# Merging the halves of 32x32 inverses: two (chunk, head) units in one 64x64 product, of which the diagonal blocks are kept

## The chip, the core and the metric

The kernel runs on one core of one Trainium2 chip. The core has a matrix engine (TensorE, "PE" in the profile, with its weight loads listed apart as "PEld"), a vector engine (VectorE, "DVE"), a scalar engine (ScalarE, "ACT"), a general engine (GpSimd, "POOL") and an engine that issues transfers (SyncE, "SP"). Each works through its own queue of instructions, and an instruction waits on semaphores for the results it needs. Matrix products are written to PSUM, here eight banks of 512 float32 columns by 128 partitions; ACT and DVE copy them out to SBUF.

The metric is the time of one execution on the device in microseconds, the median over the runs.

## The reference, cut to what matters

One layer of a hybrid decoder on 256 tokens of width 2048: a pooling mixer and an RWKV-7 time mixing side by side, an output projection, a squared-ReLU MLP and a gated embedding. The change lies in the time mixing, whose core is this recurrence over tokens, for 16 heads of size 64:

```python
def step(S, inp):
    r_t, w_t, k_t, v_t, a_t, b_t = inp
    sa = jnp.einsum('bhij,bhj->bhi', S, a_t)
    S = S * w_t[:, :, None, :] + sa[..., None] * b_t[:, :, None, :] + v_t[..., None] * k_t[:, :, None, :]
    y = jnp.einsum('bhij,bhj->bhi', S, r_t)
    return S, y
```

## The kernel before, in words

**Chunks instead of tokens.** The recurrence is computed in chunks of 64 tokens. Within a chunk, the products of all tokens with each other (the scores, tile SC) form a triangular 64x64 system per chunk and head, and its inverse is needed. The 16 heads are split into two groups, `gi` 0 and 1, of 8 heads; with 4 chunks each group has 32 (chunk, head) units.

**The inverse.** `inverse` works on a group at once. The 64x64 triangle of a unit is cut into two 32x32 diagonal blocks and one 32x32 block beside them. Both diagonal blocks lie on partitions 0 to 31 and 32 to 63: ACT copies them into `tmp` (L612), DVE transposes them into `AT` (L616), 31 steps of two DVE instructions build the inverses in `X` (L621, L625), and DVE transposes the results into `T1G` (L630, first block) and back into `tmp` (L634), from where ACT puts them into SC (L638). It is a generator: `pace` runs a step of it each time that TensorE's covering work has advanced by a given estimate.

**The merge.** `rwkv_merge` makes the block beside the diagonal. The first products, PSUM tile `gm`, multiply the score block SC[0:32, unit, 32:64] with the first inverse T1G[0:32, unit]; ACT copies the result to T1G[32:64] (L650). The second products, `qm`, multiply that with the second inverse, and ACT copies the result into SC (L657). Each is 32 products of 32x32 on 32 rows, one per unit, in two banks of 16.

**Order.** TensorE's instructions stay in the order in which the program is written (`manual_schedule` for PE alone). The other engines' queues are ordered by a scheduler from the dependencies and priorities. Between the dependent steps of the time mixing `fill(us)` puts products of the large projections, estimated in microseconds, as cover: `fill(1.5)` stands between gm and qm, and comes out as nine products of 128x512. Around the merge the program runs, for group 0: values of group 0, fill, scores of group 1 (`rwkv_scores`, L572, masked out of the banks by DVE at L579), merge of group 0, start of group 1's inverse, fill, core of group 0. For group 1: the pooling mix (`pool_mix`, L870 on ACT and L871 on DVE), merge, values, fill, core.

**Buffers.** The tiles of the time mixing come from a pool with one buffer per tag, so a tile waits until the last reader of the one before it in its tag is done. In group 0, `AT` and then `T1G` have the tag q0, `X` has q1, `tmp` q2; the values' tiles UV (written by ACT at L670 from the banks `vt`) use q0 and q1 after them. The small PSUM tiles (`rw_bank`: values, scores, gm, qm, core) share four banks. The large projections have four others. Weights are loaded by SP in tiles `raw`, split by ACT (L151, two halves) and DVE (L152, the difference) into `wh` and `wl`, three buffers each.

Of the kernel before, what the change touches and what calls it, by code (L numbers as in the profile page):

```python
# [9 lines left out]
F32 = mybir.dt.float32  # L10
F32R = mybir.dt.float32r
AF = mybir.ActivationFunctionType
# [28 lines left out]
def trunk(  # L41
# [19 lines left out]
    nc = tc.nc  # L61
# [11 lines left out]
    def rw_bank(name):  # L73
        return psr.tile([128, 512], F32, tag="rw", name=name)
# [159 lines left out]
    def fill(us):  # L234

        while us > 0 and queue:
            us -= advance()
# [42 lines left out]
    rp = rctx.enter_context(tc.tile_pool(name="rp", bufs=1))  # L280
# [58 lines left out]
    for kg, (tg, n) in enumerate((("tE", 1), ("tF", 2), ("zk", 3), ("zr", 3), ("zv", 3), ("BK", 2), ("BKt", 2))):  # L339
# [13 lines left out]
        if kg == 4:  # L353
            for tt in range(2):
                for i, q in enumerate((2, 3)):
                    nc.tensor.matmul(
                        sbank[:, tt : tt + 1], sums[q][:, 0, tt * 128 : (tt + 1) * 128], ones[:, 0:1],
                        start=i == 0 and tt == 0, stop=i == 1, skip_group_check=True,
# [242 lines left out]
    def inverse(gi, st):  # L601


        SC = st["SC"]
        SCu = SC[:, 0].rearrange("s c h t -> s (c h) t")
        tags = ("tB", "tD", "tE") if gi else ("q0", "q1", "q2")
        AT, X, tmp = (
            rp.tile([64, 32, 32], F32, tag=tg, name=f"{nm}{gi}") for nm, tg in zip(("AT", "X", "tmp"), tags)
        )
        for q in range(2):  # L610
            r = slice(q * 32, q * 32 + 32)
            nc.scalar.activation(tmp[r], SCu[r, :, q * 32 : q * 32 + 32], AF.Copy)  # L612
        nc.gpsimd.memset(X, 0.0)
        nc.gpsimd.memset(X.rearrange("u j t -> u (j t)")[:, ::33], 1.0)
        yield
        nc.vector.transpose(AT.rearrange("u s t -> u t s"), tmp.rearrange("s u t -> s t u"))  # L616
        yield
        for k in range(31):
            n, m = k + 1, 31 - k
            t_ = tmp.rearrange("u j t -> u (j t)")[:, 0 : n * m].rearrange("u (j t) -> u j t", t=m)  # L620
            nc.vector.tensor_tensor(  # L621
                t_, X[:, 0:n, k : k + 1].to_broadcast([64, n, m]),
                AT[:, k, n:32].unsqueeze(1).to_broadcast([64, n, m]), op=ALU.mult,
            )
            nc.vector.tensor_tensor(X[:, 0:n, n:32], X[:, 0:n, n:32], t_, op=ALU.add)  # L625
            yield
        T1G = rp.tile([64, 32, 32], F32, tag=tags[0], name=f"T1G{gi}")
        for hf in range(2):
            h = slice(hf * 16, hf * 16 + 16)
            nc.vector.transpose(T1G[0:32].rearrange("t u j -> t j u")[:, h], X[0:32][:, h])  # L630
            yield
        for hf in range(2):
            h = slice(hf * 16, hf * 16 + 16)
            nc.vector.transpose(tmp.rearrange("j u t -> j t u")[:, h], X.rearrange("u j t -> u t j")[:, h])  # L634
            yield
        for q in range(2):
            r = slice(q * 32, q * 32 + 32)
            nc.scalar.activation(SCu[r, :, q * 32 : q * 32 + 32], tmp[r], AF.Copy)  # L638
        st["T1G"] = T1G
        yield  # L640

    def rwkv_merge(gi, st):
        SC, T1G = st["SC"], st["T1G"]
        SCu = SC[:, 0].rearrange("s c h t -> s (c h) t")
        for hf in range(2):
            b = rw_bank("gm")
            for u in range(16):
                uu = hf * 16 + u
                nc.tensor.matmul(b[32:64, u * 32 : u * 32 + 32], SCu[0:32, uu, 32:64], T1G[0:32, uu, :], start=True, stop=True)
            nc.scalar.activation(T1G[32:64, hf * 16 : hf * 16 + 16].rearrange("t u j -> t (u j)"), b[32:64, :], AF.Copy)  # L650
        fill(1.5)
        for hf in range(2):
            b = rw_bank("qm")
            for u in range(16):
                uu = hf * 16 + u
                nc.tensor.matmul(b[0:32, u * 32 : u * 32 + 32], T1G[32:64, uu, :], SCu[32:64, uu, 32:64], start=True, stop=True)
            nc.scalar.activation(  # L657
                SCu[0:32, hf * 16 : hf * 16 + 16, 32:64], b[0:32, :].rearrange("j (u t) -> j u t", t=32), AF.Copy
            )

    def rwkv_values(gi, st, zv):

# [236 lines left out]
    fill(7.0)  # L899
    rwkv_scores(0, st0)  # L900
    beside += [inverse(0, st0), 1.65, 0.0]
    rwkv_sources(0, st0)
    finish(p_zv0)
# [8 lines left out]
    fill(7.0)  # L912
    rwkv_scores(1, st1)
    rwkv_merge(0, st0)
    beside += [inverse(1, st1), 0.95, 0.0]
    fill(1.5)
    core0 = rwkv_core(0, st0)
# [9 lines left out]
    run(beside.pop(0) if beside else ())  # L927
    beside.clear()
    rwkv_merge(1, st1)
    rwkv_values(1, st1, zv1[0])  # L930

# [423 lines left out]
```

## Time and profile before

| | |
|---|---|
| Median of 3 runs | 1205.03 us (1204.11 to 1207.36) |
| The profiled execution: span from its first to its last instruction | 1198.9 us; its own device time isn't listed, and the runs lie 5.2 to 8.5 us above this span |
| PE busy | 1179.6 us, 98% |
| PE weight loads busy | 1013.6 us, 85% |
| DVE, ACT, POOL busy | 72%, 57%, 1% |
| gm and qm products (L649, L656) | 128 records each, 191 ns each, overlapping |
| ACT copies of gm and qm (L650, L657) | 4 each, 0.59 us each |
| Scalar copy of a 32x1024 block (L612) | 1.06 us |

In the profile's timelines a row gives the start, the duration, the engine, the line, the operation, and the tile written and the tiles read; "x64" means that many records in a row, whose duration is then that of the whole stretch. In the rows by stretch, the busy time and the count of records of PE, PEld, DVE, ACT and POOL stand in that order, then the granted TensorE clock as a share of full speed, the share of the transfer engines and the GB/s.

### The profile page before, as it was taken

To read this page: it belongs to the slowest core of one execution; us is meant where nothing else is said; L and a number is where in the kernel's file an instruction comes from. 1 tells how busy PE (TensorE), PEld (TensorE's weight loads), DVE (VectorE), ACT (ScalarE), POOL (GpSimd) and SP (SyncE) were. 2 spreads that over 40 slices of the span, in tenths; PEclk is the share of its full clock that TensorE was granted. 3 is DMA by queue.
4 is the path that set the end of the run, shared out by engine and by line. 5 is a ranking of instruction groups with operands and counts; after the bars stand their busy time and mean duration, and the time that the engine had idled before them with its cause. 6 is when DMAs were issued, how large, how long until landed. Compare 5 with 4: busy or idle time off the path is not lost.

```text
span 1198.9 us, 18442 instructions
## 1 busy us (share of the span) xinstructions
PE 1179.6 (98%) x7076; PEld 1013.6 (85%) x7076; DVE 868.1 (72%) x1150; ACT 687.7 (57%) x1260; POOL 15.4 (1%) x65
## 2 busy tenths in 40 slices
PE   8999999999999999999999999999999999999996
PEld 6999988988888888888888788888888888778886
DVE  8687987854556667666888878666667888887552
ACT  6857565665545556555555555555555655668544
POOL 4000000000000000000000000000000000000000
PEclk9999999999999999999999999999999999999999
DMA  7463542354355565666665666665565655776631
GB/s 250 151 202 110 173 155 95 121 186 142 116 177 169 185 185 191 192 193 189 194 203 197 197 197 203 195 187 189 192 193 178 211 198 191 290 234 219 194 121 71
DMA packets 60328, 216.88 MB, mean 181 GB/s; under 512 B 6736, under 2 KB 7120, under 8 KB 59856
## 3 DMA queue, kind: packets, MB, share of 16 engines
q1 hardware_dynamic: 59952, 215.19, 55.1%
q8 instruction: 55, 0.90, 0.3%
q10 hardware_dynamic: 288, 0.52, 0.1%
q14 instruction: 33, 0.27, 0.1%
HBM read 213.59 MB, written 2.10 MB: 180 GB/s over the span
## 4 chain that ended last, share of the span: by engine, by line
PE 81%; DMA 6%; DVE 6%; ACT 4%; issue 2%; SPq 0%; ACTq 0%; DVEq 0%
PE u_w L986 20%; PE u_w L990 10%; DMA raw_d<-in_w_ffn_down_dram 5%; PE d_b L1101 4%; PE d_b L1100 4%; PE d_b L1102 4%; PE gt_b L173 2%; PE gt_b L175 2%; PE gt_b L174 2%; PE zv_b L164 1%; PE zp_b L173 1%; PE wag_b L333 1%; PE zv_b L165 1%; PE zv_b L166 1%; PE zp_b L175 1%
## 5 line engine op out<-in xcount | busy, mean ns | idle before, releaser
L986 PE MATMUL u_w<-h,wh_u 128*128 128x512 f32 x1024 | 355.4, 393 | 0.0
L990 PE MATMUL u_w<-h,wl_u 128*128 128x256 f32 x1024 | 285.5, 279 | 0.0
L151 ACT ACTIVATE wh_u<-raw_u 128x512 fp32r<-128x512 f32 x256 | 147.6, 624 | 162.9 <-PE u_w L986 82.0
L152 DVE TENSOR_TENSOR wl_u<-raw_u,wh_u 128x1024 fp32r<-128x1024 f32 x128 | 156.6, 1224 | 112.1 <-ACT wh_u L151 112.1
L986 PEld LDWEIGHTS u_w<-h,wh_u 128*128 128x128 f32 x1024 | 191.8, 187 | 43.2
L990 PEld LDWEIGHTS u_w<-h,wl_u 128*128 128x128 f32 x1024 | 193.1, 189 | 0.1
L152 DVE TENSOR_TENSOR wl_gt<-raw_gt,wh_gt 128x1024 fp32r<-128x1024 f32 x24 | 29.4, 1225 | 23.9 <-ACT wh_gt L151 23.9
L151 ACT ACTIVATE wh_gt<-raw_gt 128x512 fp32r<-128x512 f32 x48 | 27.8, 631 | 23.0 <-PE gt_b L175 20.4
L1140 DVE TENSOR_TENSOR td<-raw_d 128x512 f32<-128x512 f32 x22 | 15.2, 692 | 33.9 <-DMA raw_d<-in_w_ffn_down_dram 33.9
L164 PE MATMUL zv_b<-hTh,wh_zv 128*128 128x256 f32 x128 | 37.7, 294 | 0.0
L173 PE MATMUL gt_b<-wh_gt,h 128*128 128x512 f32 x96 | 37.5, 390 | 0.0
L164 PE MATMUL zr_b<-hTh,wh_zr 128*128 128x256 f32 x128 | 37.5, 293 | 0.0
L175 PE MATMUL gt_b<-wh_gt,h 128*128 128x512 f32 x96 | 37.4, 389 | 0.0
L174 PE MATMUL gt_b<-wl_gt,h 128*128 128x512 f32 x96 | 37.4, 389 | 0.0
L166 PE MATMUL zr_b<-hTh,wl_zr 128*128 128x256 f32 x128 | 37.2, 290 | 0.1
L164 PE MATMUL zk_b<-hTh,wh_zk 128*128 128x256 f32 x128 | 37.0, 289 | 0.0
L165 PE MATMUL zr_b<-hTl,wh_zr 128*128 128x256 f32 x128 | 36.9, 288 | 0.0
L165 PE MATMUL zk_b<-hTl,wh_zk 128*128 128x256 f32 x128 | 36.3, 284 | 0.5 <-DVE hTl L157 0.5
L166 PE MATMUL zk_b<-hTh,wl_zk 128*128 128x256 f32 x128 | 36.3, 284 | 0.2 <-DVE wl_zk L152 0.2
L166 PE MATMUL zv_b<-hTh,wl_zv 128*128 128x256 f32 x128 | 36.2, 283 | 0.0
L165 PE MATMUL zv_b<-hTl,wh_zv 128*128 128x256 f32 x128 | 36.2, 283 | 0.0
L156 ACT ACTIVATE wad<-raw_d 128x512 fp32r<-128x512 f32 x22 | 13.9, 632 | 36.6 <-DMA raw_d<-in_w_ffn_down_dram 34.5
(804 smaller groups left out, 3081.4 us busy)
## 6 DMA issues: line engine op xcount, KB each, us to landing
raw_u<-in_w_ffn_up_dram SPq DMA_DIRECT2D x128, 512.0 KB, 3.5
raw_d<-in_w_ffn_down_dram SPq DMA_DIRECT2D x128, 512.0 KB, 4.2
raw_gt<-in_w_ple_gate_dram SPq DMA_DIRECT2D x24, 512.0 KB, 3.5
raw_zk<-in_w_in_dram SPq DMA_DIRECT2D x16, 512.0 KB, 3.3
raw_zr<-in_w_in_dram SPq DMA_DIRECT2D x16, 512.0 KB, 3.3
raw_zv<-in_w_in_dram SPq DMA_DIRECT2D x16, 512.0 KB, 3.3
raw_zp<-in_w_in_dram SPq DMA_DIRECT2D x16, 512.0 KB, 3.2
raw_o<-in_w_out_dram SPq DMA_DIRECT2D x16, 512.0 KB, 3.5
```

Of the source, the lines that this page charges most:

```text
L151: nc.scalar.activation(wh[:, a * 512 : (a + 1) * 512], raw[:, a * 512 : (a + 1) * 512], AF.Copy)
L152: nc.vector.tensor_tensor(wl, raw, wh.bitcast(F32), op=ALU.subtract)
L164: nc.tensor.matmul(o, w_h, ah, start=first and ct % 2 == 0, stop=False, skip_group_check=True)
L165: nc.tensor.matmul(o, w_h, al, start=False, stop=False, skip_group_check=True)
L166: nc.tensor.matmul(o, w_l, ah, start=False, stop=last, skip_group_check=True)
L173: nc.tensor.matmul(o, a_h, wh[:, 0:n], start=first, stop=False)
L174: nc.tensor.matmul(o, a_h, wl[:, 0:n], start=False, stop=False)
L175: nc.tensor.matmul(o, a_l, wh[:, 0:n], start=False, stop=last)
L986: nc.tensor.matmul(bank[:, ct, :].rearrange("p (s t) -> p s t", s=2), wh[:, c], hl, start=k == 0, stop=False, skip_group_check=True,)
L990: nc.tensor.matmul(bank[:, ct, 0:T], wl[:, c], hl[:, 0, :], start=False, stop=k == 15, skip_group_check=True)
L1100: nc.tensor.matmul(banks[n], ah, wh, start=first, stop=False)
L1101: nc.tensor.matmul(banks[n], ah, wl, start=False, stop=False)
```

## The change

The merge takes two units per product. The left operand holds two 32x32 blocks side by side (64 columns), the right operand too, so the 64x64 result holds the two wanted products on its diagonal and two unwanted ones beside it. 16 products cover the 32 units, in one bank: even ones on partitions 0 to 63, odd ones on 64 to 127, eight column ranges of 64 each. Four copies then take the diagonal blocks out: block row r goes to every fourth unit from r on; r 0 and 2 are copied by ACT, 1 and 3 by DVE, 32 partitions by 8x32 elements each.

So that two neighbouring units lie side by side, the score block is first copied by ACT to a place of its own, `A12`, on partitions 64 to 95 of X's buffer (tiles of 96 partitions instead of 64); the first inverse's transposition goes to T1G[64:96] beside it.

```diff
@@ -605,8 +605,11 @@
         SCu = SC[:, 0].rearrange("s c h t -> s (c h) t")
         tags = ("tB", "tD", "tE") if gi else ("q0", "q1", "q2")
         AT, X, tmp = (
-            rp.tile([64, 32, 32], F32, tag=tg, name=f"{nm}{gi}") for nm, tg in zip(("AT", "X", "tmp"), tags)
+            rp.tile([96, 32, 32], F32, tag=tg, name=f"{nm}{gi}") for nm, tg in zip(("AT", "X", "tmp"), tags)
         )
+        A12, AT, X, tmp = X[64:96], AT[0:64], X[0:64], tmp[0:64]
+        nc.scalar.activation(A12, SCu[0:32, :, 32:64], AF.Copy)
+        st["A12"] = A12
         for q in range(2):
             r = slice(q * 32, q * 32 + 32)
             nc.scalar.activation(tmp[r], SCu[r, :, q * 32 : q * 32 + 32], AF.Copy)
@@ -624,10 +627,10 @@
             )
             nc.vector.tensor_tensor(X[:, 0:n, n:32], X[:, 0:n, n:32], t_, op=ALU.add)
             yield
-        T1G = rp.tile([64, 32, 32], F32, tag=tags[0], name=f"T1G{gi}")
+        T1G = rp.tile([96, 32, 32], F32, tag=tags[0], name=f"T1G{gi}")
         for hf in range(2):
             h = slice(hf * 16, hf * 16 + 16)
-            nc.vector.transpose(T1G[0:32].rearrange("t u j -> t j u")[:, h], X[0:32][:, h])
+            nc.vector.transpose(T1G[64:96].rearrange("t u j -> t j u")[:, h], X[0:32][:, h])
             yield
         for hf in range(2):
             h = slice(hf * 16, hf * 16 + 16)
@@ -642,21 +645,30 @@
     def rwkv_merge(gi, st):
         SC, T1G = st["SC"], st["T1G"]
         SCu = SC[:, 0].rearrange("s c h t -> s (c h) t")
-        for hf in range(2):
-            b = rw_bank("gm")
-            for u in range(16):
-                uu = hf * 16 + u
-                nc.tensor.matmul(b[32:64, u * 32 : u * 32 + 32], SCu[0:32, uu, 32:64], T1G[0:32, uu, :], start=True, stop=True)
-            nc.scalar.activation(T1G[32:64, hf * 16 : hf * 16 + 16].rearrange("t u j -> t (u j)"), b[32:64, :], AF.Copy)
+        A12 = st["A12"]
+
+        def block_products(name, left, right, place):
+
+            b = rw_bank(name)
+            for q in range(16):
+                u = slice(2 * q, 2 * q + 2)
+                nc.tensor.matmul(
+                    b[q % 2 * 64 : q % 2 * 64 + 64, q // 2 * 64 : q // 2 * 64 + 64], left(u), right(u),
+                    start=q < 2, stop=True, skip_group_check=True,
+                )
+            for r in range(4):
+                src = b[r * 32 : r * 32 + 32].rearrange("t (m j) -> t m j", j=64)[:, :, r % 2 * 32 : r % 2 * 32 + 32]
+                if r % 2:
+                    nc.vector.tensor_copy(place[:, r::4], src)
+                else:
+                    nc.scalar.activation(place[:, r::4], src, AF.Copy)
+
+        def two(t_):
+            return t_.rearrange("u b j -> u (b j)")
+
+        block_products("gm", lambda u: two(A12[:, u]), lambda u: two(T1G[64:96, u]), T1G[32:64])
         fill(1.5)
-        for hf in range(2):
-            b = rw_bank("qm")
-            for u in range(16):
-                uu = hf * 16 + u
-                nc.tensor.matmul(b[0:32, u * 32 : u * 32 + 32], T1G[32:64, uu, :], SCu[32:64, uu, 32:64], start=True, stop=True)
-            nc.scalar.activation(
-                SCu[0:32, hf * 16 : hf * 16 + 16, 32:64], b[0:32, :].rearrange("j (u t) -> j u t", t=32), AF.Copy
-            )
+        block_products("qm", lambda u: two(T1G[32:64, u]), lambda u: SCu[32:64, u, 32:64], SCu[0:32, :, 32:64])
 
     def rwkv_values(gi, st, zv):
 
```

## The prediction

> **What bounds the kernel now.** First the page: the busy times and the chain that ended last.
>
> ```profile
> PE 1179.6 (98%) x7076; PEld 1013.6 (85%) x7076; DVE 868.1 (72%) x1150; ACT 687.7 (57%) x1260; POOL 15.4 (1%) x65
> ...
> PE 81%; DMA 6%; DVE 6%; ACT 4%; issue 2%; SPq 0%; ACTq 0%; DVEq 0%
> ```
>
> TensorE has work almost all the time and carries four fifths of the chain. Second, the view of waits, for PE alone, longest first:
>
> ```profile
> PE wag_b L333 <- ACT tA_t L314: 5.0, 1, 5.0
> PE h3t L1007 <- DVE x L1120: 1.3, 1, 1.3
> ```
>
> After the start no wait of PE is above 1.3 us, and none is in the merge. PE's order is written out by hand, so time that a merge product gives back moves everything behind it forward, and time that PE waits moves everything back. Third, the two merges stage by stage (us of the stretch, then busy time of PE, PEld, DVE, ACT, POOL, the clock). The first three rows are group 0 (first products gm, nine covering products of a projection, second products qm), the others group 1.
>
> ```profile
> 186.04:188.18 2.14, 2.14 (x66) 2.10 (x64) 1.29 (x2) 0.59 (x1) 0.00 (x0) 1.00 0.76 245
> 188.18:190.45 2.27, 2.27 (x13) 1.62 (x10) 0.00 (x0) 2.14 (x4) 0.00 (x0) 1.00 0.03 11
> 190.45:192.58 2.13, 2.13 (x65) 2.09 (x64) 1.55 (x2) 2.08 (x4) 0.00 (x0) 1.00 0.00 0
> 259.98:262.11 2.13, 2.13 (x65) 2.09 (x64) 0.89 (x2) 1.17 (x3) 0.00 (x0) 1.00 0.92 264
> 262.11:264.40 2.29, 2.29 (x13) 1.61 (x10) 0.48 (x1) 1.06 (x2) 0.00 (x0) 1.00 0.00 0
> 264.40:266.53 2.13, 2.13 (x65) 2.09 (x64) 0.79 (x1) 1.66 (x3) 0.00 (x0) 1.00 0.00 0
> ```
>
> Each block of 32 products is 64 PE records (a float32 product shows as two) and takes 2.13 us of PE. Only four such blocks exist, 8.5 us in all, so the change can win no more than a part of that; it can lose more if PE waits in one of the gaps.
>
> **The products.** Each block becomes 16 products of 64x64, 32 records, on alternating column halves. The trace has no such product on 32 rows; nearest are these (PE in time order: start, us, line):
>
> ```profile
> 200.21 0.68 PE L736 MATMUL sm<-UV,BKt 128*64 128x64 f32 x16
> 200.73 1.10 PE L749 MATMUL rym<-UV,SC 128*64 128x64 f32 x16
> 201.75 0.39 PE L164 MATMUL zv_b<-hTh,wh_zv 128*128 128x256 f32 x1
> ```
>
> L736 alternates column halves: 16 records in 0.52 us. L749 writes one half only: 16 records in 1.02. For 32 records that is 1.04 or 2.04. I take 1.05, because the new products alternate as L736 does, and keep 2.04 as the other end. Alone, four blocks would save 4 x 1.08 = 4.3 us.
>
> **What stands around them in group 0.** These are DVE and then ACT in the stretch of the merge, before:
>
> ```profile
> 186.15 1.29 DVE L579 TENSOR_TENSOR SC<-sc,cmask 128x512 f32<-128x512 f32 x2 [0.73 <-PE sc L572]
> 191.03 1.23 DVE L152 TENSOR_TENSOR wl_zv<-raw_zv,wh_zv 128x1024 fp32r<-128x1024 f32 x1 [3.60 <-ACT wh_zv L151]
> 192.18 2.16 DVE L616 STREAM_TRANSPOSE AT<-tmp 64x1024 f32<-64x1024 f32 x1
> ```
>
> ```profile
> 187.28 0.59 ACT L650 ACTIVATE T1G<-gm 32x512 f32<-32x512 f32 x1 [3.11 <-PE gm L649]
> 188.29 0.59 ACT L650 ACTIVATE T1G<-gm 32x512 f32<-32x512 f32 x1 [0.43 <-PE gm L649]
> 188.90 1.06 ACT L612 ACTIVATE tmp<-SC 32x1024 f32<-32x1024 f32 x1
> 189.87 1.13 ACT L151 ACTIVATE wh_zv<-raw_zv 128x512 fp32r<-128x512 f32 x2
> 191.03 1.06 ACT L612 ACTIVATE tmp<-SC 32x1024 f32<-32x1024 f32 x1
> 192.10 0.59 ACT L657 ACTIVATE SC<-qm 32x512 f32<-32x512 f32 x1
> 192.75 0.59 ACT L670 ACTIVATE UV<-vt 64x512 f32<-64x512 f32 x1
> ```
>
> Now both gm copies come first on ACT and end at 188.9, well before qm at 190.45; copying tmp out and transposing it (group 1's inverse) come later and nobody waits for them. The built order of the changed program differs in four ways.
>
> First, gm takes one bank, and it is the one that the last score products have just filled, since the values' second bank now stays taken until gm has run (A12 lies in X's buffer, which UV needs next). So gm waits for the first L579: 186.15 plus half of 1.29, 186.8, and starts at about 186.9 instead of 186.04: 0.85 us of PE lost. gm ends at 187.94, the nine covering products (2.27) at 190.2.
>
> Second, ACT's queue ahead of the first gm copy now holds the new A12 copy of group 1 (same size as L612, 1.06; it waits for the second L579, 187.44), one UV copy (0.59), the two wh_zv halves (1.13) and the other UV copy (0.59). From 187.5 that makes 190.9.
>
> Third, the four gm copies form a chain. They write interleaved slices of one tile, and each waits for the one before it: ACT, DVE, ACT, DVE. Their size is 32x256 from a bank; rows of 256 per partition are the nearest:
>
> ```profile
> L297 ACT ACTIVATE zk_t<-zk_b,omu x8: 450/460/473, 53.5 to 138.1; 128x256 f32<-128x256 f32 x8
> ```
>
> ```profile
> 162.02 0.46 DVE L298 SCALAR_TENSOR_TENSOR zr_t<-zr_b,par_sb,zr_t 128x255 f32<-128x255 f32 x1
> ```
>
> I take 0.46 for each on either engine.
>
> Fourth, in between stand group 1's steps: on ACT both tmp copies lie between the first and the third copy, on DVE the wl_zv difference before the second and the L616 transposition, which needs tmp, before the fourth. So: first copy 190.9 to 191.35; second, behind wl_zv (190.4 to 191.6), to 192.05; both tmp copies to 193.35; third to 193.8; L616 193.4 to 195.55; fourth to 196.0. The second qm product needs the fourth copy. PE, done with its cover at 190.2, starts qm in earnest at 196.05, waits 5.8 us, and ends qm at 197.1. Before it ended at 192.58: **4.5 us later**. My bounds are 3.7 (copies of 0.3, hand-overs free) and 5.2.
>
> What is late next: behind qm ACT has UV, the qm copies (again four in a chain), and wh_zv; by the same durations the last qm copy ends at about 201.8, and the um products that read it come at 202.0, so nothing more is lost, with 0.2 us to spare (an estimate; 0.5 if it fails). Group 1's inverse starts about 1 us later on DVE, while PE is 4.5 later: it stays ahead.
>
> **Group 1.** The copies stand together here, but behind the mp copies:
>
> ```profile
> 259.68 0.88 ACT L870 ACTIVATE mp<-pm,par_sb 128x256 fp32r<-128x256 f32 x2 [0.56 <-DVE mp L871]
> ...
> 262.83 0.47 ACT L870 ACTIVATE mp<-pm,par_sb 128x256 fp32r<-128x256 f32 x1
> ```
>
> The last L870, before at 262.83, now precedes the gm copies and waits for the third L871 on DVE (about 261.1), so it ends at 261.6. gm ends at 259.98 + 1.05 = 261.03. The chain of four then takes 4 x 0.46 and hand-overs: 263.5. PE's cover ends at 261.03 + 2.29 = 263.3. PE waits 0.2 and ends qm at 264.55 instead of 266.53: **2.0 us earlier**. If a copy took 0.6, 1.5.
>
> **Edits with no cost on the path.** Group 0's A12 copy (1.06 on ACT) stands near 100 us, and ACT still waits for PE some us later:
>
> ```profile
> 106.95 0.47 ACT L297 ACTIVATE zv_t<-zv_b,omu 128x256 f32<-128x256 f32 x1 [0.67 <-PE zv_b L166]
> ```
>
> That wait and the next ones take it up; if that cover were gone, 1.06. One half of the last transposition of X (L634) is moved on DVE from 149 us to about 168.6, ahead of the score banks' release, and the scores have two banks instead of three:
>
> ```profile
> 172.83 1.16 PE L572 MATMUL sc<-AR,BK 64*128 64x128 f32 x16
> ...
> 174.03 1.29 DVE L579 TENSOR_TENSOR SC<-sc,cmask 128x512 f32<-128x512 f32 x2 [0.67 <-PE sc L572]
> ```
>
> The next scores follow 4.0 us after these; the masks end at 175.3, 1.5 us ahead. The first scores at 172.83 keep less, since half a transposition (half of L616's 2.16) now runs before the step that frees their bank: I estimate 0.7. If both covers failed, 1 us. The DMA queue and POOL's queue hold the same instructions in the same order.
>
> **The clock.** PE has no wait this long before, apart from both ends of the kernel, and these show what follows. At the end (PE's last product ends at 1189.9; the clock is the number before the DMA share):
>
> ```profile
> 1189.00:1190.00 1.00, 0.89 (x8) 0.69 (x6) 0.00 (x0) 0.07 (x1) 0.00 (x0) 1.00 0.00 0
> 1193.00:1194.00 1.00, 0.00 (x0) 0.00 (x0) 0.96 (x3) 0.93 (x2) 0.00 (x0) 0.69 0.00 0
> 1194.00:1195.00 1.00, 0.00 (x0) 0.00 (x0) 0.08 (x1) 0.40 (x1) 0.00 (x0) 0.50 0.46 184
> ```
>
> A mean of 0.69 in that us puts the fall to 0.50 at 1193.4, 3.5 us after the last product. At the start (L333 asked for stretches: the first us of work, then 9 to 10):
>
> ```profile
> L333 PE MATMUL wag_b<-wag,tA_t x3: 687/688/850, 5.0 to 6.2; 128*128 128x288 f32 x3
> ```
>
> ```profile
> L333 PE MATMUL wag_b<-wag,tA_t x5: 406/406/602, 8.6 to 9.7; 128*128 128x288 f32 x5
> ```
>
> The first products take 0.69, those from about 9.0 on 0.41: slow for 3.9 us after PE's first work. A wait of 5.8 us exceeds 3.5, so I expect the clock to fall near 193.9 and some 3.9 us at half rate after 196.05, which lose half of that, **1.9 us**. Bounds: 0 (no fall) and 3 (a slow stretch half as long again).
>
> [...]
>
> **The sum**, on the profiled span of 1198.9: + 4.5 - 2.0 + 1.9 = + 4.4 us. That execution's own device time isn't listed; the median of the runs, 1205.03, is 6.1 above the span. I predict 1205.03 + 4.4 = **1209.4 us**.
>
> **The rivals.**
> - The same waits, but the clock holds. For it: one lone qm product can run at 192.1, when the second copy is done, and splits the wait into 1.9 and 3.8 us, and 3.8 is hardly over 3.5. Against it: two records hardly make a busy PE. 1205.03 + 2.5 = 1207.5.
> - Column halves don't overlap on 32-row products: blocks at 2.04 as in L749. Group 0 loses 1.0 more in qm and 0.35 through the UV copy that waits for gm, group 1 2.0. With the clock's fall 1212.8. Against it stands L736, whose halves do overlap.
> - Not slower: the copies come through before 190.2, so that qm never waits. Then group 0 saves 0.2 in gm and 1.1 in qm, group 1 2.0 to 2.1: - 3.4, 1201.6; with gm's bank free as well, 1200.7. It decides where the chain's end falls under 190.2, that is with tmp copies and L616 (2.1 + 2.2) out of the chain and ACT's queue before it 1 us shorter. Against it: both engines work through their queues in order in every row above.
>
> **How the numbers follow.** The forecast 0.47 (own range 1208 to 1211), the clock that holds 0.28 (1206 to 1208.6), no overlap 0.15, not slower 0.10. No change that a measurement of this kernel can tell is within 0.3%, 3.6 us: 1201.4 to 1208.65. Slower takes 0.42 of the forecast, 0.14 of no overlap and 0.06 of the clock that holds; faster takes 0.07 of the last case; the rest, 0.31, is the same. The range 1206.0 to 1213.0 leaves out the last case and some of the edges.
>
> **What would show it.** In the profile after: 32 gm records in 1.05 us, starting 0.85 us after the last scores (if at once, the bank wait is wrong); a PE wait of 5 to 6 us before the second qm product in group 0, put down to DVE's T1G copy (the main step; if under 2 us, the chain is wrong); qm of group 1 some 2 us nearer its gm; a clock under 1.00 for some us near 195 to 200. Wrong altogether it is if ACT or DVE take the copies sooner than their place in the queue, or if the scores stall on two banks.

## The result, and the profile after

The changed kernel takes 1210.25 us (median of 22 runs, 1204.85 to 1214.5); the kernel before, run beside it, 1204.4 us (22 runs). The ratio is **1.0041, 95% interval 1.0029 to 1.0052**: slower by 4.9 us (3.5 to 6.3); the two medians lie 5.9 us apart. One later run of the kernel with the wait filled (experiment 1), 1462.38 us at a mean clock of 0.753, is left out of every figure of that kernel. The prediction was 1209.4 us with 1206.0 to 1213.0, and slower as the likeliest side.

The profiled execution of the changed kernel, from its page: busy time of the engines, then the granted clock in forty slices of 30 us.

```profile
span 1206.4 us, 18198 instructions
PE 1183.2 (98%) x6948; PEld 1014.8 (84%) x6948; DVE 872.8 (72%) x1158; ACT 689.1 (57%) x1262; POOL 15.4 (1%) x65
PEclk9999997999999999999999999999999999999998
```

PE has 128 records fewer and is busy for 3.6 us more, although the new products are shorter: the seventh slice (181 to 211 us) has a granted clock of 0.7. The view of waits says what stands ahead of it:

```profile
PE qm L655 <- DVE T1G L662: 5.2, 2, 3.5
PE gm L655 <- DVE SC L579: 0.8, 1, 0.8
```

The two merges stage by stage, in the same columns as before (us, then PE, PEld, DVE, ACT, POOL, the clock, the transfer engines). Group 0: the wait before gm, gm, the nine covering products, the wait, qm. Group 1: gm, cover, qm.

```profile
186.09:186.87 0.78, 0.00 (x2) 0.00 (x1) 0.75 (x2) 0.00 (x0) 0.00 (x0) 1.00 0.70 179
186.87:187.95 1.08, 1.08 (x33) 1.01 (x33) 0.54 (x1) 0.50 (x1) 0.00 (x0) 1.00 0.89 353
187.95:190.28 2.33, 2.33 (x13) 1.60 (x9) 0.10 (x1) 2.29 (x5) 0.00 (x0) 1.00 0.05 12
190.28:195.82 5.54, 0.30 (x4) 0.19 (x3) 3.97 (x5) 3.34 (x5) 0.00 (x0) 0.76 0.25 95
195.82:197.72 1.90, 1.90 (x31) 1.78 (x31) 1.66 (x8) 0.00 (x0) 0.00 (x0) 0.50 0.00 0
269.01:270.08 1.07, 1.07 (x33) 1.00 (x32) 0.87 (x2) 0.58 (x2) 0.00 (x0) 1.00 0.76 237
270.08:272.37 2.29, 2.29 (x14) 1.61 (x10) 1.27 (x4) 1.22 (x3) 0.00 (x0) 1.00 0.27 109
272.37:273.57 1.20, 1.20 (x33) 1.13 (x32) 0.08 (x1) 1.05 (x2) 0.00 (x0) 1.00 0.00 0
```

A block takes 1.07 to 1.20 us where it took 2.13. In group 1 that is the whole story: 4.56 us from gm to the end of qm instead of 6.55. In group 0, 5.5 us lie between the cover and the rest of qm, and qm itself runs at half clock. Who holds it is seen in ACT's and then DVE's timeline:

```profile
187.45 1.05 ACT L611 ACTIVATE X<-SC 32x1024 f32<-32x1024 f32 x1 [3.31 <-DVE SC L579]
188.41 0.57 ACT L682 ACTIVATE UV<-vt 64x512 f32<-64x512 f32 x1
188.99 1.15 ACT L151 ACTIVATE wh_zv<-raw_zv 128x512 fp32r<-128x512 f32 x2
190.17 0.59 ACT L682 ACTIVATE UV<-vt 64x512 f32<-64x512 f32 x1
190.77 0.37 ACT L664 ACTIVATE T1G<-gm 32x256 f32<-32x256 f32 x1
191.17 2.12 ACT L615 ACTIVATE tmp<-SC 32x1024 f32<-32x1024 f32 x2
193.32 0.38 ACT L664 ACTIVATE T1G<-gm 32x256 f32<-32x256 f32 x1
```

```profile
191.44 0.42 DVE L662 COPY T1G<-gm 32x256 f32<-32x256 f32 x1
193.32 1.98 DVE L619 STREAM_TRANSPOSE AT<-tmp 64x1024 f32<-64x1024 f32 x1 [1.47 <-ACT tmp L615]
195.34 0.43 DVE L662 COPY T1G<-gm 32x256 f32<-32x256 f32 x1
```

gm is ready at 187.95. The four copies (0.4 us each, 1.6 in all) end at 195.8, because 3.3 us of other work stand ahead of the first on ACT, tmp's two copies ahead of the third, and the transposition that needs tmp ahead of the fourth on DVE.

**A yardstick without the noise of whole runs.** Whole executions of one kernel scatter by several us, before the merge and in the MLP behind it (in the changed kernel the last scores end at 186.09, 188.7 and 189.3 us, and from h2t to the end it takes 841.9 to 849.9). From the end of the last scores to a fixed product behind them they hardly do. The products used are um (products of the core, which read the merged inverse), vt (the values of group 1) and h2t (the MLP's input). The table gives such distances as differences to the kernel before, worked out from the start times in PE's timelines (before: scores end at 186.11, first um at 197.53, first vt of group 1 at 266.53, first h2t at 355.23). Three profiles of the changed kernel agree to 0.12 us, two of the filled wait to 0.04.

| kernel | after gm | after qm | first um | group 1: first vt | h2t |
|---|---|---|---|---|---|
| changed kernel, three profiles | -0.2 | +5.1, +5.2 | +9.1 | +7.1, +7.1, +7.2 | +7.1, +7.1, +7.2 |
| wait filled, two profiles | -0.2 | +4.6 | +4.6 | +3.3 | +3.3 |
| change in group 1 alone | 0.0 | 0.0 | 0.0 | -1.7 | -1.7 |
| A12 in tmp | -1.1 | +0.5 | +1.6 | -0.5 | -0.5 |
| copies first | -0.2 | -0.4 | +0.2 | -1.5 | -1.5 |
| both edits | -1.1 | -1.9 | -1.5 | -3.3 | -2.8 |
| both edits, no alternation | -0.3 | -0.6 | -0.6 | -1.0 | -1.1 |

### The profile page after: what moved, and what is told of

It is laid out like the page before. It is cut to its first block, busy times and chain, and to the rows that moved or that the text cites. A ratio compares the mean times of both kernels' runs of the same rounds, so it can differ in the third digit from the quotient of the medians.

```text
span 1206.4 us, 18198 instructions
## 1 busy us (share of the span) xinstructions
PE 1183.2 (98%) x6948; PEld 1014.8 (84%) x6948; DVE 872.8 (72%) x1158; ACT 689.1 (57%) x1262; POOL 15.4 (1%) x65
## 4 chain that ended last, share of the span: by engine, by line
PE 85%; DVE 6%; DMA 4%; ACT 4%; issue 1%; SPq 0%; ACTq 0%; DVEq 0%
PE u_w L998 20%; PE u_w L1002 10%; PE d_b L1113 6%; PE d_b L1114 6%; PE d_b L1112 6%; DMA raw_d<-in_w_ffn_down_dram 2%; PE gt_b L173 2%; PE gt_b L174 2%; PE gt_b L175 2%; PE zp_b L173 1%; PE zv_b L164 1%; PE zp_b L175 1%; PE zp_b L174 1%; PE d_w L1113 1%; PE d_w L1114 1%
## 5 line engine op out<-in xcount | busy, mean ns | idle before, releaser
L998 PEld LDWEIGHTS u_w<-h,wh_u 128*128 128x128 f32 x1024 | 192.0, 187 | 44.9
```

The costliest lines, as they stand in the source:

```text
L998: nc.tensor.matmul(bank[:, ct, :].rearrange("p (s t) -> p s t", s=2), wh[:, c], hl, start=k == 0, stop=False, skip_group_check=True,)
```

## The experiments

**1. The wait filled with work (wait kept, clock kept).**

```diff
             b = rw_bank(name)
+            if name == "qm" and gi == 0:
+                for i in range(24):
+                    nc.tensor.matmul(b, hT_h[0][:, 0:128], hT_h[0][:, 0:512], start=True, stop=True, skip_group_check=True)
             for q in range(16):
```

> The changed kernel, but between the cover and the second products of group 0 stand 24 extra products of 128x512 into the bank that qm then overwrites (they compute nothing that is used). They need nothing that is late, so they fill the wait on the chain of copies with work: 24 x 0.227 = 5.45 us from 190.2, about as long as the 5.2 us that PE waited. My theory (the wait costs 4.3 us, and the clock that falls in it costs some more): no wait over 0.5 us before qm, a clock of 1.00 throughout, and the time is that of the two merges' waits alone, + 4.3 - 2.0 = + 2.3 us on the kernel before, ratio 1.0019. Rival (the clock costs little in most runs, and the waits are the whole loss): as the changed kernel, 1.0035 to 1.0045.

Measured: 1.0038 (1.0020 to 1.0056). PE's timeline of it, and its waits around the merge:

```profile
189.65 5.60 PE L655 MATMUL qm<-hTh 128*128 128x512 f32 x24
195.18 1.55 PE L658 MATMUL qm<-SC,T1G 32*64 32x64 f32 x32
```

```profile
PE gm L658 <- DVE SC L579: 0.8, 1, 0.8
PE um L742 <- DVE SC L665: 0.7, 1, 0.7
```

The chain ends as late as before, but the clock stays at 1.00 from 186 to 210 us, and the distances shrink from + 7.1 to + 3.3. So in the profiled executions the late chain alone leaves the kernel 3.3 us behind at h2t, with group 1's gain already taken off, and the clock adds 3.8. Something not expected appears as well: um waits 0.7 us for the last qm copy. In the changed kernel that wait is hidden, because the covering products ahead of it run at half speed (from 198.31 us on one starts each 0.43 us, ahead of qm each 0.23). The ratio did not follow: it came out where the rival had it, though its interval also holds + 3.3 us (1.0027).

**2. Both timed again on one chip.** The kernels are the changed one and that of experiment 1, unaltered.

> The changed kernel, timed on one chip beside the kernel with the filled wait. So far both lie near 1.004, with intervals too wide to tell them apart, while the profiles part them by 3.8 us (from the last scores to the end of the projections: + 7.1 for the changed kernel, + 3.3 with the wait filled). The mean clock of a run's record says how long it was slow: (1 - clock) x 2 x span. In the 22 runs of the changed kernel so far that is 18.4 us in the mean, of the kernel before some 8.7, and the profiled run with 24 us is the slowest of them. My theory (every run loses the clock after the wait, for 2 to 4 windows of 3.41 us, and the profiled ones are the long ones): a mean clock of 0.990 to 0.994 in all runs, and a time 1.5 to 3.5 us above the filled wait, ratio 1.0035 to 1.005. Rival (the fall costs nothing in the time): the same time as the filled wait within 1 us.

> The filled wait (24 extra products before qm of group 0) once more, beside the changed kernel. My theory: a mean clock as that of the kernel before, 0.995 to 0.998, and + 3.3 us on the kernel before, ratio 1.002 to 1.0035. Rival: as the changed kernel, 1.004.

Measured: 1.0061 (1.0038 to 1.0085) and 1.0055 (1.0036 to 1.0075). The profiles repeat the + 7.2 and + 3.3, but the whole times don't part the two, as the rival of the first expectation had it, and + 3.3 us now lies outside the filled wait's interval. From h2t to the end the filled wait took 847.1 and 851.0 us in its two profiles, the changed kernel 844.1, 841.9 and 849.9, the kernel before 843.7; every queue has the same order there in both. Part of it is a wait near the end of the MLP:

```profile
PE pp_b L173 <- ACT pp L1234: 1.7, 1, 1.7
```

In the changed kernel that wait is 0.2 to 0.6. So what the clock cost by h2t is at least partly not seen in the end time; why the stage behind is longer with the wait filled is open.

The clocks did come out as expected (the windows of 3.41 us in the expectation are the steps that experiment 7 cuts out of the traces). In 29 runs of the changed kernel the mean clock is 0.990 to 0.994, in 73 runs of the kernel before and 17 with the wait filled 0.994 to 0.998. Counted as (1 - clock) x 2 x span that is 18.6 us of half rate against 8.6 and 8.7, so the changed kernel loses 10.0 us more in the mean. Of its 29 runs 21 lie below 0.994, the lowest value of the kernel before, and 8 on it, where 3 of the 73 lie: most of its runs lose the clock, and that every one does is not shown. The first profiled one, with 0.990, was among the longest.

**3. The change in group 1 alone.** Group 0 keeps the old merge, T1G[0:32] and no A12.

```diff
+        if gi == 0:
+            ...
+            return
         A12 = st["A12"]
```

> The change in group 1 alone; group 0 keeps the old merge, its tiles and no A12. My theory: group 1 gains 2.0 us as it did in the profile (from + 9.0 us at gm to + 7.0 at the values' products), and nothing else is lost: - 2.0 us, ratio 0.9983, and group 0's share of the loss is the difference to the changed kernel, some 7 us. Rival (the loss is not only in group 0; A12's copy, the moved transposition, or what follows group 1 costs too): 1.000 or above.

Measured: 0.9975 (0.9958 to 0.9991). Between the first um of group 0 and the first vt of group 1 it gains 1.7 us, and from gm to vt of group 1 2.0, as the changed kernel does. So by the profile the whole loss is in group 0, and group 1 keeps its gain by itself.

**4. A12 in tmp's buffer.** X's buffer is then free for the values as in the kernel before.

```diff
-        A12, AT, X, tmp = X[64:96], AT[0:64], X[0:64], tmp[0:64]
+        A12, AT, X, tmp = tmp[64:96], AT[0:64], X[0:64], tmp[0:64]
```

> The changed kernel with A12 on partitions 64 to 95 of tmp's buffer instead of X's, in both groups. X's buffer is then free for the values as before, so the UV copies stand ahead of the merge, the bank of gm is free, and ACT's queue ahead of the first gm copy is empty. My theory (the place of A12 makes the bank wait and puts the UV copies, A12's copy and the weights' copies ahead of the first gm copy): gm starts 0.8 us earlier, straight after the last scores; the chain's end moves from 195.8 to about 191.4 and the wait of PE before qm from 5.2 to about 2 us, too short for the clock to fall; group 0 ends near its old time, and with group 1's - 2.0 the whole is - 2 us, ratio 0.998. Rival (group 1's tmp copies and its transposition make the wait, wherever A12 lies): a wait of 4 us or more and 1.002 or above.

Measured: 0.9998 (0.9979 to 1.0016). The steps are as expected: gm follows the scores at once (- 1.1 us after gm instead of - 0.2), and the wait before qm is 1.9 us. But the clock falls all the same, which I had excluded (an estimate from the 3.5 us for which it held behind the last product of the kernel before); the windows in experiment 7 show it. From qm to um 1.2 us are lost (+ 0.5 after qm, + 1.6 at um), with no wait of PE there. In the 12 runs the half rate comes to 12.0 us in the mean, counted as above, 3.4 more than before.

**5. Copies first.** A12 stays in X's buffer.

```diff
             for r in range(4):
                 ...
-                if r % 2:
-                    nc.vector.tensor_copy(place[:, r::4], src)
-                else:
-                    nc.scalar.activation(place[:, r::4], src, AF.Copy)
+                with tc.high_priority(30000):
+                    if r % 2:
+                        nc.vector.tensor_copy(place[:, r::4], src)
+                    else:
+                        nc.scalar.activation(place[:, r::4], src, AF.Copy)
```

> The changed kernel with a high scheduling priority on the eight copies of each merge, A12 where the change puts it. Only A12's copy of group 1 stays ahead of the first gm copy, and one UV copy and half of a weights' copy between the first and the third; tmp's copies and the transposition come behind the chain. My theory (the chain's place in the queues of ACT and DVE is the loss): the bank wait of 0.8 us before gm stays, the chain ends at about 190.9, PE waits 0.7 us and keeps its clock; group 0 ends 0.7 us earlier than before, group 1 2.0: - 2.7 us, ratio 0.9978. Rival (the hand-overs of four copies in a chain are slow by themselves): a wait of 2 us or more, ratio 0.999 or above.

Measured: 0.9976 (0.9959 to 0.9993). PE's waits from 180 to 300 us:

```profile
PE gm L655 <- DVE SC L579: 0.8, 1, 0.8
PE qm L655 <- DVE T1G L663: 0.5, 1, 0.5
PE um L740 <- ACT R L726: 0.4, 1, 0.4
```

With the same products, the same four hand-overs and the same bank wait, the wait before qm goes from 5.2 to 0.5 us and the clock stays (mean 0.997 in the profiled run, 0.990 in that of the changed kernel). So neither the hand-overs nor the number of copies made the wait, but their place in the two queues. The profile has - 1.5 us at h2t and not the - 2.7 expected: the end of qm gains 0.4 instead of 0.7, and 0.6 are lost from there to um, 0.4 of it in a wait for R's copy; the interval of the ratio holds both.

**6. Both edits, the same without alternation, and more cover.**

> The changed kernel with both edits: A12 in tmp's buffer, and the high priority on the copies. My theory: gm starts straight after the last scores, the chain of four copies ends under the nine covering products, PE waits less than 0.3 us before qm, the clock stays at 1.00. Then all four blocks give their 1.08 us: - 4.2 us from the end of the last scores to the end of group 1's core if nothing behind qm waits, - 3.5 if um waits for R or for the last qm copy as it did in the runs so far (0.4 to 0.7); ratio 0.9965 to 0.997. Rival (the two edits mend the same wait, and do not add): - 2.7 us, 0.9976 as with the priority alone.

Measured: **0.9969 (0.9957 to 0.9982)**, 1201.57 us against 1203.81 (medians). The two edits add: - 1.9 us at the end of qm, - 3.3 at the values of group 1. Between um and h2t some of it goes again (0.4 at the first um, where R's copy is behind one of tmp; 0.4 in group 1's core). This is the fastest form found that keeps the change in both groups; beside group 1 alone (0.9975) and the copies first (0.9976) its lead is inside the intervals.

```diff
-            for q in range(16):
+            for q in (*range(0, 16, 2), *range(1, 16, 2)):
```

> The kernel of both edits, but the 16 products of a block in another order: the eight on the lower column half first, then the eight on the upper. All products, operands, copies and queues stay. My theory (the halves overlap only where neighbours alternate, as L736 against L749): a block takes about 2.0 us instead of 1.06, group 0 and group 1 each lose 2 us, and the time is that of the kernel before, 0.999 to 1.001, some 4 us above the kernel of both edits. Rival (half as many products are half the time, whatever their order): as the kernel of both edits.

Measured: 1.0001 (0.9985 to 1.0016). The first block in PE's timeline, without and (second fence) with alternation:

```profile
185.92 1.89 PE L655 MATMUL gm<-T1G,tmp 32*64 32x64 f32 x32
```

```profile
186.36 1.15 PE L655 MATMUL gm<-T1G,tmp 32*64 32x64 f32 x32
```

Taken up one column half and then the other, the same 16 products take 1.89 us; alternating they take 1.15. In the table the first block gains 1.06 us with alternation and 0.31 without (after gm): 0.75 of the 1.06 us come from the order, the rest from the smaller number. The time loses 1.8 us at h2t rather than the 4 that I had put down, because the block takes 1.89, not 2.04, and 0.4 each at um and in group 1's core are lost in the kernel of both edits and not here.

```diff
-        fill(1.5)
+        fill(1.5 if gi else 7.0)
         block_products("qm", ...
```

> The changed kernel with the queues as they are, but fill(7.0) instead of fill(1.5) between gm and qm of group 0: 36 covering products, about 7.3 us, taken from later fills. The chain of copies still ends near 195. My theory (PE's wait and the clock are the loss, not work): the bank wait of 0.8 stays, qm waits under 0.5, the clock stays at 1.00, and the products' gain comes through: + 0.83 - 1.08 - 1.08 in group 0, - 2.0 in group 1, - 3.3 us in all, or - 2.6 if um waits for the last qm copy (0.7); ratio 0.9973 to 0.998. Rival (the chain is only pushed back by more work in the queues, since the weights' copies of that cover come ahead of it): a wait of 2 us or more before qm, 1.000 or above.

Measured: 0.9984 (0.9969 to 0.9999). There is no wait before qm and no fall of the clock behind the merge (mean 0.997 in the profiled run); um waits 1.0 us for a qm copy. By h2t, where the cover taken early is made good, it is 2.2 us ahead of the kernel before. Work that waits for nothing cures the loss as well as a better place in the queues does.

**7. What sets the slow spell.** First the changed kernel once more, for a second profile:

> The changed kernel once more, for a second profile of it. In the first profile the clock was at 0.50 from 193.2 for 13.7 us. [...] Rival (the spell follows from the wait alone): again 13 to 14 us.

Measured: 1208.57 us in one run; again 0.8 and 5.2 us of wait, again a spell of 13.7 us (195.9 to 209.6), as in the profile of experiment 2. The rival had it, as far as this goes, though the mean clocks of the runs say 10.0. The spells read here, though, are multiples of 3.41 us (3.41, 10.2 and 13.65), in steps that one grid of 3.41 us per execution fits. In the kernel before, the trace's record of the clock has 133.12 us, 39.0 steps, from the return near 9 us to the fall at 142.07; in the changed kernel the same 133.12 to a fall at 142.0, one step at 0.50, and 47.79 us, 14.0 steps, to the fall at 193.2. The last fall, behind PE's end, lies 0.1 us beside the grid in both. So the windows were cut at the falls. In order: the kernel before (a spell that I had overlooked), A12 in tmp, and the changed kernel.

```profile
138.65:142.07 3.42, 3.31 (x29) 3.10 (x28) 3.32 (x8) 3.40 (x7) 0.00 (x0) 1.00 0.06 24
142.07:145.48 3.41, 3.41 (x18) 3.41 (x18) 3.27 (x11) 1.88 (x5) 0.00 (x0) 0.50 0.78 243
```

```profile
190.35:193.76 3.41, 1.49 (x25) 1.00 (x25) 1.65 (x2) 3.35 (x5) 0.00 (x0) 1.00 0.04 14
193.76:197.17 3.41, 3.41 (x22) 2.81 (x19) 2.99 (x6) 1.70 (x4) 0.00 (x0) 0.50 0.41 144
197.17:198.00 0.83, 0.83 (x5) 0.38 (x4) 0.76 (x4) 0.57 (x2) 0.00 (x0) 1.00 0.00 0
```

```profile
189.83:193.24 3.41, 0.75 (x5) 0.22 (x3) 1.64 (x2) 3.34 (x5) 0.00 (x0) 0.99 0.23 82
193.24:196.65 3.41, 0.83 (x16) 0.83 (x18) 3.16 (x6) 0.43 (x2) 0.00 (x0) 0.50 0.18 72
196.65:200.06 3.41, 3.41 (x26) 2.81 (x23) 2.57 (x10) 1.55 (x3) 0.00 (x0) 0.50 0.01 2
200.06:203.47 3.41, 3.41 (x22) 2.57 (x21) 1.94 (x4) 1.52 (x3) 0.00 (x0) 0.50 0.00 0
203.47:206.87 3.40, 3.40 (x16) 2.25 (x16) 3.13 (x10) 0.74 (x2) 0.00 (x0) 0.50 0.44 154
206.87:210.28 3.41, 3.41 (x66) 3.08 (x64) 1.38 (x4) 2.53 (x5) 0.00 (x0) 1.00 0.02 5
```

The busy time doesn't say when the clock comes back: in the changed kernel three whole windows are busy before it does, in A12 in tmp one. What parts these four is how much of a window the large products (256 or 512 columns) fill. By the start times in the timelines: 196.65 to 200.06 has 2.34 us of them (0.69), the next 1.79 (0.52), the one up to 206.87 about 2.7 (0.80), and there the clock returns; in A12 in tmp 193.76 to 197.17 has 2.63 (0.77), and it returns at once. The rest of those windows are qm and the small products of the core. The fall in the kernel before came with PE busy for 3.31 of 3.42 us, of which 1.84 were these:

```profile
139.27 1.84 PE L493 MATMUL kkn<-jhead,tF_t 128*128 128x2 f32 x16
```

Large products fill some 0.4 of that window. But for the fall the share is no rule: with the wait filled, late in the MLP, a window of that execution's grid (36 steps ahead of the fall at 1199.23, behind PE's end) kept the clock with PE busy for 1.83 us, of which large products make some 0.9 (0.28):

```profile
1076.35:1079.76 3.41, 1.83 (x14) 1.33 (x12) 2.83 (x4) 2.89 (x7) 0.00 (x0) 1.00 0.43 130
```

To test the share for the return, the changed kernel got large products behind qm instead of the core's small ones:

```diff
-    fill(1.5)
+    fill(6.0)
     core0 = rwkv_core(0, st0)
```

> The changed kernel with fill(6.0) instead of fill(1.5) behind the merge of group 0: after qm come 36 large covering products (about 11 us at half rate) before the small products of the core. The profiles so far show the clock at 0.50 for spells of 3.4 us (before, near 142; A12 in tmp, from 193.8) and of 13.7 us (the changed kernel, twice), all multiples of 3.41. My theory (the clock is set at the ends of windows of 3.41 us that run freely, by how much of the window large products fill; it returned at the end of windows filled to 0.77 and 0.82, and not after one filled to 0.69): the same wait of about 5 us, but the second or third window after the fall is full, so the spell is 6.8 or 10.2 us. Rival (the spell follows from the length of the wait alone): 13.7 us again.

Measured: 1210.55 us in one run, the same waits up to qm, and a spell of 10.2 us, three windows. The moved cover made a new wait of 1.4 us in group 1, and with it a second spell of one window. The windows of both, cut at the falls:

```profile
194.28:197.70 3.42, 1.07 (x20) 1.08 (x22) 3.22 (x7) 0.23 (x1) 0.00 (x0) 0.50 0.21 83
197.70:201.11 3.41, 3.41 (x22) 2.81 (x19) 2.57 (x10) 1.55 (x3) 0.00 (x0) 0.50 0.00 0
201.11:204.52 3.41, 3.41 (x9) 2.64 (x9) 1.97 (x4) 1.52 (x3) 0.00 (x0) 0.50 0.00 0
279.62:283.03 3.41, 3.41 (x13) 2.52 (x12) 0.43 (x2) 2.74 (x5) 0.00 (x0) 0.50 0.16 60
```

```profile
281.46 2.67 PE L432 MATMUL bsum<-tF_t,jsum 128*128 128x512 f32 x4
```

With the same wait before qm the spell is 10.2 us instead of 13.7, so its length does not follow from the wait alone, as far as one run shows. The share does not hold either. The large products start at 198.52, so they fill 0.76 of the second window (no return) and all of the third (return); but in the window from 279.62 they start at 281.46 and fill 0.46, and the clock returns at its end. The rest of that window are the products of the values, 128x128. So neither measure tells which windows end a spell; that is open, for the return as for the fall. The time of this run tells nothing of the spell, because of the new wait.

## Why the prediction was right, step by step

- **Products.** 1.05 us a block was predicted, 1.07 to 1.20 was measured at full clock; the rival without overlap (2.04) fell, and experiment 6 shows that the overlap needs the alternating order (1.15 us a block with it, 1.89 without).
- **Bank wait before gm.** 0.85 predicted, 0.8 in the view of waits and 0.85 in the table (- 0.2 after gm); experiment 4 removes it by A12's place alone, as argued.
- **The chain.** First copy at 190.9 predicted, 190.77 measured; end 196.0 predicted, 195.77 measured; a wait of 5.8 predicted, 5.2 in two pieces beside the lone product at 192.0. The end came 0.2 early: ACT's queue was through 0.13 sooner, the transposition took 1.98 rather than 2.16, and the first and the last copy 0.37 and 0.43 rather than 0.46. Against that stood a slip of 0.1 in the prediction: two copies of tmp, 1.06 each, end at 193.47 and not at 193.35 when they start at 191.35. Its lower bound of 3.7 doesn't follow from copies of 0.3 either, since only the first and the last lie on the path (0.3 less, so 4.2, and the hand-overs). qm's end was put at + 4.5; with the wait filled it is + 4.6, in the changed kernel + 5.1 at half clock. Experiments 3, 4 and 5 bear out the place and the cause. The rival "not slower" named its condition (tmp's copies and the transposition out of the chain, and a shorter queue ahead of it), and experiments 5 and 6 came near it: - 1.5 and - 2.8 at h2t against its - 3.4.
- **Behind qm "nothing more lost, with 0.2 us to spare".** Wrong: um waits 0.7 for the last qm copy as soon as the clock holds, where the step allowed 0.5 for its failure. In the changed kernel itself that copy ends at 203.5 instead of 201.8, and the slow cover hides it.
- **Group 1.** - 2.0 predicted, - 2.0 measured (from + 9.1 to + 7.1), and the same alone.
- **Edits with no cost** (A12's copy in group 0, the moved transposition, two score banks): the first scores start at 172.81 against 172.83 and the last end at 186.09 against 186.11, so none in the first profile, though one mask came 0.6 us late (174.65). The two later profiles, whose scores end at 188.7 and 189.3, scatter by more than these edits could cost.
- **The clock.** The fall was put near 193.9 and came at 193.2. The term was mis-sized: 3.9 us at half rate after the restart were put down, worth 1.9. In the profiled execution it was 11.0 us, worth 3.8 by h2t. The step took its 3.9 from the start of the kernel; after qm two windows passed with PE busy throughout before a third brought the clock back, and why is open (experiment 7). In the mean of 29 runs the clock is slow for 10.0 us more than in the kernel before, instead of the 6.0 that the step implies (2.1 left of the wait, 3.9 after it). What that costs at the end of the kernel isn't settled: by experiments 1 and 2 the filled wait is not measurably faster.
- **The sum.** + 4.4 predicted. The profiles have + 4.6 for group 0, + 0.7 at um, - 2.0 for group 1 and + 3.8 for the clock, + 7.1 by h2t. The 22 runs had + 4.9 (3.5 to 6.3), six later ones 1.0061, + 7.3 (4.6 to 10.2). The side, the wait and both groups were right for the reasons given; that 4.4 lies within 0.5 us of 4.9 is partly luck, since two terms were too small by 2.6 us together and the first runs don't show it. The clock that holds was a rival at 0.28; no run shows it clearly.

## What to carry to other kernels

In this kernel a product that is cut to half its time paid only where its copies got out of the queues by the end of the cover (or the cover was made longer): price such copies by their place in each engine's built order, not by their 0.4 us, and look at which buffer the new operand sits in. Emptying the bank with both ScalarE and VectorE made a chain through two queues here, with 5.2 us of wait, and 0.5 once the copies stood first in both. Where two column halves are used, alternate them product by product (1.15 us a block against 1.89 here).

## What the runs showed that was not expected

- The clock fell after a wait of 1.9 us in one execution (experiment 4) and held after a wait of 1.6 us in another (the window from 1076.35 with the wait filled). It fell after a stretch with PE busy for 3.31 of 3.42 us too, near 142 us of the kernel before; such a spell of one step, from 142.0 to 152.3 us on, is there in four profiles (the kernel before, the changed kernel's first one and that of experiment 2, the second with the wait filled). The prediction counted waits alone.
- The half rate comes in whole steps of 3.41 us (one, three or four here). PE busy throughout a step did not end it in three of the steps cut here and did in five, and neither the busy time nor the share of large products tells which.
- The filled wait has the better profile by 3.8 us up to the MLP and no better time; the cause is open.
